# Turning the queries and keys of local attention: a product with the identity in place of the transposing instruction

## The chip, the cores and the metric

The kernel runs on one core of a Trainium2 chip. A core has a matrix engine (TensorE; PE in the profile, with its loads of the stationary operand shown apart as PEld), a vector engine (DVE), an activation engine (ACT), a general engine (POOL) and DMA queues, of which SP issues most here. The metric is the device time of one execution in microseconds.

## The reference, cut to what matters

One layer of a hybrid encoder: a normed input is projected, and three groups of heads work on it side by side, a chunked state-space scan, attention in a window, and attention to a memory. Their outputs are joined and projected back. There are two sequences, of 1024 and of 256 tokens, with 2048 features, handled as ten tiles of 128 tokens. The part that matters here is the attention in a window, with 8 query heads and 2 key heads of 64 features:

```python
q = rms_norm(q.reshape(b, T, ATT_HEADS, ATT_HEAD_DIM), q_norm_g)
k = rms_norm(k.reshape(b, T, ATT_KV_HEADS, ATT_HEAD_DIM), k_norm_g)
...
s = jnp.einsum('bnqgrd,bnkgd->bngrqk', qb, kw).astype(jnp.float32) * (d ** -0.5)
...
logits = jnp.where(valid[:, None, None], s - slopes[None, :, :, None, None] * dist[:, None, None], -jnp.inf)
...
o = jnp.einsum('bngrqk,bnkgd->bnqgrd', probs.astype(v.dtype), vw)
```

The sum over d needs the features of q and k on the partitions, while the projection leaves tokens there. So each tile of q and of k has to be turned.

## The kernel before

The large projections run all through the kernel: weight tiles are fetched, split into a rounded high part and a rounded low part by `wsplit` (L206 on ACT, L207 on DVE), and multiplied in the rounded kind (type `F32R`), three products for each pair of parts. `block_tok` (L258 to L260) has tokens on the output's partitions, `block_feat` (L293 to L295) features, with 320 moving columns, and `block_pair` (L1268 to L1270) saves products by sums of parts.

The smaller work is written as generators: `k_prep` for a tile's keys, `attn` for a tile's window attention, `mem_attn`, `ssd_up`, `ssd_down` and so on. They stand in two lanes; after each step of a projection, `pump` takes so many steps from the lanes, by the rates in `RATES`. That is the order in which the program is written down. The order in which each engine then gets its instructions is made by a planner of the language from this order, from the priorities that the kernel gives (`tc.high_priority`, `tc.issue_after`), from the buffers that are free and from the planner's own costs of instructions.

`k_prep(t)` fetches a tile's keys, norms them and writes `kh`: 128 partitions by 4 x 2 x 64, the high part of each key head twice side by side and the low part twice, all in the rounded type (L528, L530). Then four turns of 128 x 128 (L536) fill one bank `pk`, and `kT` (high, L539 on DVE) and `kL` (low, L540 on ACT) are copied from it. `attn(t)` does the same for queries: for each of the two key heads it writes `qh` (L647, L648: high and low part of four query heads, side by side), turns it in four instructions (L653) into the bank `pq`, and copies it to `qT` (L655 on ACT). In `scores` (L671, L672) one product takes the turned high and low part of a query together, as 128 rows, against the doubled high part of the keys, and a second one against the low part.

`identr` is the 128 x 128 identity in the rounded type. Other turns of the kernel use the same transposing instruction: in the rounded type L744, L853, L889, L1074 and L1088, in the unrounded type L449, L610, L611, L693, L794 and L1038. Unrounded products are in `values` (L703, L809), in the sums of `dt_prep` (L590 to L592) and in `diag` (L970).

Of the kernel before, what the change touches and what calls it, by code (L numbers as in the profile page):

```python
# [11 lines left out]
F32R = mybir.dt.float32r  # L12
# [7 lines left out]
P = 128  # L20
# [24 lines left out]
def hymba_encoder_kernel(  # L45
# [7 lines left out]
    V, A, G, T, S = nc.vector, nc.scalar, nc.gpsimd, nc.tensor, nc.sync  # L53
# [23 lines left out]
    def const(shape, name, dtype=F32):  # L77
        return cp.tile(shape, dtype, tag=name, name=name)
# [4 lines left out]
    def psum(name):  # L83
        return mix.tile([P, 512], F32, tag="mix", name=name)


    identr = const([P, P], "identr", F32R)
# [34 lines left out]
    def rsqrt(dst, src, scale, n):  # L122
        G.tensor_scalar(out=dst, in0=src, scalar1=scale, scalar2=EPS, op0=ALU.mult, op1=ALU.add)
        G.tensor_tensor(out=dst, in0=dst, in1=mhalf[:, :n], op=ALU.pow)

    def hv(ap, n=8):
        return ap.rearrange("p (h d) -> p h d", h=n)

    def hb(ap, n, d):
        return ap.unsqueeze(2).broadcast_to([P, n, d])  # L130
# [284 lines left out]
    def w2(name):  # L415
        return mp.tile([P, 512], F32, tag="wa", name=name, bufs=WA)
# [86 lines left out]
    def taken(name, t):  # L503
        return fetched.pop((name, t)) if (name, t) in fetched else fetch[name](t)

    def fetch_next():

        name = lanes[0][1][0] if len(lanes[0]) > 1 else ("", 0)
        if name[0] in fetch:
            fetched[name] = fetch[name[0]](name[1])  # L510

    def k_prep(t):
        r = taken("k_prep", t)
        yield
        ss = sm.tile([P, 2], F32, tag="s2", name="kss", bufs=4)
        sq = w2("ksq")[:, :P]
        A.activation(sq, r, AF.Square)
        V.reduce_sum(out=ss, in_=hv(sq, 2), axis=AX.X)
        rr = sm.tile([P, 2], F32, tag="s2", name="krr", bufs=4)
        rsqrt(rr, ss, 1.0 / 64, 2)  # L520
        yield
        r3 = hv(r, 2)
        V.tensor_mul(r3, r3, hb(rr, 2, 64))
        V.tensor_mul(r3, r3, gq.unsqueeze(1).broadcast_to([P, 2, 64]))

        kh = mp.tile([P, 4, 2, 64], F32R, tag="wa", name="kh", bufs=WA)
        for d in range(2):
            A.activation(kh[:, 0:2, d, :], r3, AF.Copy)  # L528
        for d in range(2):
            V.tensor_sub(kh[:, 2:4, d, :], r3, kh[:, 0:2, 0, :].bitcast(F32))  # L530
        yield
        yield
        ps = psum("pk")
        kf = kh.rearrange("p a b d -> p (a b d)")
        for a in range(4):
            T.transpose(ps[:, a * P:(a + 1) * P].bitcast(F32R), kf[:, a * P:(a + 1) * P], identr)  # L536
        sl = t if t < 5 else t - 3
        c = slice(sl * P, (sl + 1) * P)
        V.tensor_copy(kT[:, :, c], hv(ps[:, :256], 2))  # L539
        A.activation(kL[:, :, c], hv(ps[:, 256:], 2), AF.Copy)  # L540
        fetch_next()
        yield
# [77 lines left out]
    def attn(t):  # L620
# [23 lines left out]
        for b in range(2):  # L644
            qh = mp.tile([P, 4, 2, 64], F32R, tag="wa", name="qh", bufs=WA)
            qb = q3[:, 4 * b:4 * b + 4, :]
            A.activation(qh[:, :, 0, :], qb, AF.Copy)  # L647
            V.tensor_sub(qh[:, :, 1, :], qb, qh[:, :, 0, :].bitcast(F32))  # L648
            yield
            ps = psum("pq")  # L650
            qf = qh.rearrange("p a b d -> p (a b d)")
            for a in range(4):
                T.transpose(ps[:, a * P:(a + 1) * P].bitcast(F32R), qf[:, a * P:(a + 1) * P], identr)  # L653
            o = mp.tile([P, 512], F32R, tag="qT", name="qT", bufs=2)
            A.activation(o, ps, AF.Copy)  # L655
            qT.append(o)
# [826 lines left out]
    def refill_o(grp, when):  # L1483
        def f(k):
            if k not in when:
                return []
            q = when[k]
            need((attn, mem_attn, ssd_down, ssd_down)[q], range(grp * 5, grp * 5 + 5))
            return [part(fill_direct, q, j, oT_d[q][grp][:, j, :],
                         gain=None if q < 2 else vec[:, R_SG + 4 * (q - 2) + j:R_SG + 4 * (q - 2) + j + 1])  # L1490
                    for j in range(4)]
        return f
# [76 lines left out]
    for u, unit in enumerate(units):  # L1569
# [43 lines left out]
    run(block_tok(w_kv, 5, ev_dtkv(0), before_last=lambda _: need(vectors, [0])), RATES[0]["kv"], hold=5,  # L1613
        extra=lambda k: some_left() if left else None)
    queue(0, k_prep, range(5))
    queue(0, attn, range(4))
    queue(1, dt_prep, [0])

# [22 lines left out]
    def gate(name, c, after=None):  # L1641
        for b in range(2):
            feat(name, b, ev_gateT(c, 1, 2 * b), 1, after if b else None)

    need(attn, range(4))
    kv_shift()
    run(block_tok(w_kv, 5, ev_dtkv(5)), RATES[1]["kv"], extra=lambda k: some_left() if left else None)
    queue(0, k_prep, range(5, 10))
    queue(0, attn, [4])
    queue(1, dt_prep, [5])  # L1650
# [110 lines left out]
```

## Time and profile before

| what | value |
|---|---|
| median of 3 runs | 1787.72 us (1787.32 to 1790.27) |
| span of the profiled execution, first to last instruction | 1784.2 us |
| PE busy | 1774.6 us, 10838 products |
| PEld busy | 1606.3 us |
| DVE busy | 1245.8 us |
| ACT busy | 921.5 us |
| POOL busy | 547.3 us |
| the four turns of L536, L653 | 40 records of 238 ns mean, 80 of 246 ns mean |

The page lists busy time by engine, then the span in slices, the DMA queues, the chain of work that ended last and the costliest groups of instructions. "L653 PE MATMUL pq<-identr,qh" means line 653 of the kernel, run on PE, that writes the tile `pq` from `identr` and `qh`. Records of the matrix engine overlap: the length of a product's record contains the way through the array, so what one costs in a stream is read from the distance of the starts and not from the lengths.

### The profile page before, as it was taken

To read this page: it belongs to the slowest core of one execution; us is meant where nothing else is said; L and a number is where in the kernel's file an instruction comes from. 1 tells how busy PE (TensorE), PEld (TensorE's weight loads), DVE (VectorE), ACT (ScalarE), POOL (GpSimd) and SP (SyncE) were. 2 spreads that over 40 slices of the span, in tenths; PEclk is the share of its full clock that TensorE was granted. 3 is DMA by queue.
4 is the path that set the end of the run, shared out by engine and by line. 5 is a ranking of instruction groups with operands and counts; after the bars stand their busy time and mean duration, and the time that the engine had idled before them with its cause. 6 is when DMAs were issued, how large, how long until landed. Compare 5 with 4: busy or idle time off the path is not lost.

```text
span 1784.2 us, 31407 instructions
## 1 busy us (share of the span) xinstructions
PE 1774.6 (99%) x10838; PEld 1606.3 (90%) x10838; DVE 1245.8 (70%) x2358; ACT 921.5 (52%) x2049; POOL 547.3 (31%) x900
## 2 busy tenths in 40 slices
PE   9999999999999999999999999999999999999999
PEld 7889999999998999999889977877988888899999
DVE  5596788888768887777665666557777644766665
ACT  5555455555434766756464565544447533533333
POOL 0105789999810100001001010000100000057775
PEclk9999999999999999999999999999999999999999
DMA  8654454445446644453635645557777764744442
GB/s 299 191 183 125 135 154 148 141 146 159 126 144 205 199 134 139 135 162 110 189 118 175 193 148 160 168 158 249 229 229 242 247 189 140 224 147 142 148 142 78
DMA packets 208207, 301.12 MB, mean 169 GB/s; under 512 B 19568, under 2 KB 86192, under 8 KB 208048
## 3 DMA queue, kind: packets, MB, share of 16 engines
q1 hardware_dynamic: 207904, 299.06, 54.5%
q8 instruction: 85, 1.39, 0.3%
q14 instruction: 74, 0.61, 0.1%
q10 hardware_dynamic: 144, 0.06, 0.0%
HBM read 236.36 MB, written 62.69 MB: 168 GB/s over the span
## 4 chain that ended last, share of the span: by engine, by line
PE 82%; issue 6%; DVE 4%; DMA 4%; POOL 2%; ACT 1%; SPq 0%; POOLq 0%; ACTq 0%; DVEq 0%
PE acc L258 9%; PE acc L260 8%; PE acc L259 8%; PE acc L1268 7%; PE acc L1270 7%; PE acc L1269 7%; PE acc L293 5%; PE acc L295 5%; PE acc L294 5%; PE accm L1268 3%; PE accm L1269 3%; PE accm L1270 3%; PE po L703 1%; PE ppt L693 1%; PE py L970 1%
## 5 line engine op out<-in xcount | busy, mean ns | idle before, releaser
L207 DVE TENSOR_TENSOR wl<-wraw,wh 128x512 fp32r<-128x512 f32 (+1 forms) x480 | 346.2, 723 | 244.0 <-ACT wh L206 238.5
L206 ACT ACTIVATE wh<-wraw 128x512 fp32r<-128x512 f32 (+1 forms) x480 | 292.2, 613 | 312.4 <-PE acc L260 147.8
L258 PE MATMUL acc<-wh,xH 128*128 128x512 f32 (+1 forms) x1088 | 418.9, 385 | 0.4 <-DVE v_all L337 0.4
L260 PE MATMUL acc<-wh,xL 128*128 128x512 f32 (+1 forms) x1088 | 410.1, 377 | 0.0
L259 PE MATMUL acc<-wl,xH 128*128 128x512 f32 (+1 forms) x1088 | 409.7, 377 | 0.0
L258 PEld LDWEIGHTS acc<-wh,xH 128*128 128x128 f32 x1088 | 204.5, 188 | 37.8 <-issue 3.4
L260 PEld LDWEIGHTS acc<-wh,xL 128*128 128x128 f32 x1088 | 204.4, 188 | 37.0 <-issue 0.2
L259 PEld LDWEIGHTS acc<-wl,xH 128*128 128x128 f32 x1088 | 204.7, 188 | 35.9 <-issue 1.6
L293 PE MATMUL acc<-xH,wh 128*128 128x320 f32 x640 | 202.8, 317 | 0.0
L294 PE MATMUL acc<-xL,wh 128*128 128x320 f32 x640 | 198.8, 311 | 0.0
L295 PE MATMUL acc<-xH,wl 128*128 128x320 f32 x640 | 198.0, 309 | 0.0
L206 ACT ACTIVATE sh<-ws 128x384 fp32r<-128x384 f32 x176 | 91.3, 523 | 204.8 <-POOL ws L1236 102.5
L207 DVE TENSOR_TENSOR sl<-ws,sh 128x384 fp32r<-128x384 f32 x176 | 123.8, 706 | 94.6 <-ACT sh L206 94.4
L1236 POOL TENSOR_TENSOR ws<-wraw 128x128 f32<-128x128 f32 x176 | 110.8, 630 | 205.8 <-DMA wraw<-in_w_in_pairs_dram 80.9
L665 POOL COPY lg<-nsink 128x2 f32<-128x2 f32 x40 | 13.6, 340 | 379.1 <-PE ppt L693 221.3
L1236 POOL TENSOR_TENSOR ws<-wraw,ws 128x128 f32<-128x128 f32 x176 | 118.7, 674 | 13.8
L293 PEld LDWEIGHTS acc<-xH,wh 128*128 128x128 f32 x640 | 120.2, 188 | 2.8 <-issue 2.2
L294 PEld LDWEIGHTS acc<-xL,wh 128*128 128x128 f32 x640 | 120.3, 188 | 1.7 <-issue 1.4
L295 PEld LDWEIGHTS acc<-xH,wl 128*128 128x128 f32 x640 | 120.2, 188 | 0.6 <-issue 0.5
L1236 POOL TENSOR_TENSOR wraw<-wraw 128x128 f32<-128x128 f32 x176 | 112.9, 642 | 13.7
L1236 POOL TENSOR_TENSOR ws<-ws,wraw 128x128 f32<-128x128 f32 x176 | 115.6, 657 | 0.0
L362 DVE SCALAR_TENSOR_TENSOR c<-u,vec,c 128x638 f32<-128x638 f32 (+1 forms) x96 | 90.0, 938 | 9.9 <-ACT c L357 9.5
(437 smaller groups left out, 3942.7 us busy)
## 6 DMA issues: line engine op xcount, KB each, us to landing
wraw<-in_w_in_laid_dram SPq DMA_DIRECT2D x176, 256.0 KB, 3.0
wraw<-in_w_in_pairs_dram SPq DMA_DIRECT2D x112, 256.0 KB, 2.7
wraw<-in_w_out_laid_dram SPq DMA_DIRECT2D x64, 256.0 KB, 3.5
wraw<-in_w_out_pairs_dram SPq DMA_DIRECT2D x64, 256.0 KB, 2.8
rf<-ac SPq DMA_DIRECT2D x40, 256.0 KB, 4.1
rb<-ac SPq DMA_DIRECT2D x40, 256.0 KB, 4.7
wraw<-in_w_mem_laid_dram SPq DMA_DIRECT2D x32, 256.0 KB, 4.4
xst<-in_x_sample_dram SPq DMA_DIRECT2D x20, 256.0 KB, 5.9
```

Of the source, the lines that this page charges most:

```text
L206: a = A.activation(h, raw, AF.Copy)
L207: b = V.tensor_sub(l, raw, h.bitcast(F32))
L258: T.matmul(ps[t][:, :n], sh, h[:, :n], start=(k_ == 0), stop=False)
L259: T.matmul(ps[t][:, :n], sh, l[:, :n], start=False, stop=False)
L260: T.matmul(ps[t][:, :n], sl, h[:, :n], start=False, stop=(k_ == KT - 1))
L293: T.matmul(o, sh, cur["H", q][:, m, c], start=(k == 0), stop=False)
L294: T.matmul(o, sh, cur["L", q][:, m, c], start=False, stop=False)
L295: T.matmul(o, sl, cur["H", q][:, m, c], start=False, stop=(k == KT - 1))
L1236: G.tensor_tensor(out=o, in0=x, in1=y, op=op)
L1268: T.matmul(ps[p], h, xh, start=(k_ == 0), stop=False)
L1269: T.matmul(ps[p], h, xl, start=False, stop=False)
L1270: T.matmul(ps[p], l, xh, start=False, stop=(k_ == 7))
```

## The change

Eight instructions of the text, two loops over four, are written in another way: in place of the transposing instruction stands an ordinary product with `kf` or `qf` as stationary operand and the identity as moving operand. The result goes to the bank in its own type, so that the type is no longer reinterpreted. Data, tiles, copies behind it and all other turns of the kernel stay.

```diff
@@ k_prep
         ps = psum("pk")
         kf = kh.rearrange("p a b d -> p (a b d)")
         for a in range(4):
-            T.transpose(ps[:, a * P:(a + 1) * P].bitcast(F32R), kf[:, a * P:(a + 1) * P], identr)
+            T.matmul(ps[:, a * P:(a + 1) * P], kf[:, a * P:(a + 1) * P], identr, start=True, stop=True)
         sl = t if t < 5 else t - 3
@@ attn
             ps = psum("pq")
             qf = qh.rearrange("p a b d -> p (a b d)")
             for a in range(4):
-                T.transpose(ps[:, a * P:(a + 1) * P].bitcast(F32R), qf[:, a * P:(a + 1) * P], identr)
+                T.matmul(ps[:, a * P:(a + 1) * P], qf[:, a * P:(a + 1) * P], identr, start=True, stop=True)
             o = mp.tile([P, 512], F32R, tag="qT", name="qT", bufs=2)
```

## The prediction

> **What bounds the kernel now.** I read the page's first parts, then the busy time in stretches of 100 us over the part of the span in which the two edited lines run, then those lines themselves.
>
> ```profile
> span 1784.2 us, 31407 instructions
> PE 1774.6 (99%) x10838; PEld 1606.3 (90%) x10838; DVE 1245.8 (70%) x2358; ACT 921.5 (52%) x2049; POOL 547.3 (31%) x900
> PEclk9999999999999999999999999999999999999999
> ```
>
> ```profile
> 500.00:600.00 100.00, 99.31 (x575) 88.26 (x574) 81.73 (x174) 50.30 (x118) 13.34 (x20) 1.00 0.64 190
> 600.00:700.00 100.00, 99.51 (x693) 93.35 (x693) 79.11 (x180) 66.34 (x168) 9.56 (x15) 1.00 0.48 147
> 700.00:800.00 100.00, 99.96 (x721) 93.43 (x720) 75.19 (x171) 61.44 (x149) 8.04 (x14) 1.00 0.50 149
> 800.00:900.00 100.00, 98.74 (x674) 90.44 (x673) 70.14 (x162) 54.64 (x141) 7.88 (x9) 1.00 0.49 144
> 900.00:1000.00 100.00, 99.94 (x633) 90.58 (x632) 66.21 (x142) 58.89 (x154) 8.23 (x16) 1.00 0.49 155
> 1000.00:1100.00 100.00, 100.00 (x570) 81.69 (x569) 62.13 (x139) 58.09 (x141) 9.69 (x16) 1.00 0.54 171
> 1100.00:1200.00 100.00, 100.00 (x527) 79.89 (x526) 55.98 (x131) 53.03 (x133) 8.26 (x17) 1.00 0.52 161
> 1200.00:1300.00 100.00, 98.94 (x612) 83.60 (x610) 73.72 (x162) 47.00 (x115) 9.02 (x24) 1.00 0.73 231
> ```
>
> The columns after the length are the busy time of PE, PEld, DVE, ACT and POOL, then the granted clock. PE is idle for 0.69 + 0.49 + 0.04 + 1.26 + 0.06 + 0 + 0 + 1.06 = 3.6 us of these 800 us, while DVE never passes 82 and ACT never passes 67 of 100. So PE sets the pace through the whole stretch, and what one instruction adds to PE's stream is added to the end. But a busy PE says little of an instruction's price, since records overlap. The price of an instruction is the distance between starts, so I go to the order of time.
>
> ```profile
> L536 PE MATMUL pk<-identr,kh x40: 222/233/282, 565.2 to 1000.1; 128*128 128x128 f32 x40
> L653 PE MATMUL pq<-identr,qh x80: 221/247/627, 624.2 to 1269.3; 128*128 128x128 f32 x80
>   ACT qT L655: 0.3, 1
> ```
>
> The edit touches 40 + 80 = 120 instructions, between 565 and 1269 us. The last row is from the list of those that waited for L653: one wait of 0.3 us in all, so the copies behind the turns have slack and a later turn of some tenths of a us starts no chain there. In time one group of four turns looks like this:
>
> ```profile
> 623.62 0.31 PE L295 MATMUL acc<-xH,wl 128*128 128x320 f32 x1
> ...
> 624.06 0.31 PE L295 MATMUL acc<-xH,wl 128*128 128x320 f32 x1
> 624.21 0.46 PE L653 MATMUL pq<-identr,qh 128*128 128x128 f32 x4
> 624.50 0.38 PE L293 MATMUL acc<-xH,wh 128*128 128x320 f32 x1
> 624.72 0.30 PE L294 MATMUL acc<-xL,wh 128*128 128x320 f32 x1
> 624.86 0.31 PE L295 MATMUL acc<-xH,wl 128*128 128x320 f32 x1
> ```
>
> The columns are start, length, engine, line and so on. Undisturbed, products of 320 columns start 0.147 us apart (three steps from 623.62 to 624.06, and 0.15 from 624.06 to 624.21). From 624.06 to 624.72 there are 0.66 us; two such products account for 0.294 of them, so four turns cost 0.366 us, **0.091 us each**, and that includes the longer step behind them (0.22 in place of 0.147).
>
> **The change part by part.** It removes 120 turns in the transposing kind and adds 120 ordinary products with the data as stationary part and the rounded identity of 128 columns as moving part. Instruction count, operands, output tile and the copies that read it stay (L539, L540, L655 read the same 512 columns); no DMA, no wait and no engine is added. So there are two terms: the price of 120 products, and what the planner, which orders each engine's instructions by its own idea of their cost, does with a different instruction.
>
> First term. No ordinary rounded product with 128 moving columns stands in the trace, so it is bounded by neighbours. What differs in the records is the load of the stationary part:
>
> ```profile
> L653 PEld LDWEIGHTS pq<-identr,qh 128*128 128x128 f32 x80 | 8.4, 140 | 1.4 <-issue 0.5
> L294 PEld LDWEIGHTS acc<-xL,wh 128*128 128x128 f32 x640 | 120.3, 188 | 1.7 <-issue 1.4
> L809 PEld LDWEIGHTS pmo<-mpT,mv 128*128 128x128 f32 x160 | 19.5, 191 | 0.9 <-ACT mpT L798 0.3
> ```
>
> A load takes 140 ns in the transposing kind, 188 in the rounded ordinary one, 191 in the unrounded one. The next rows say what that does to the distance of starts when the moving part is short.
>
> ```profile
> 834.75 0.29 PE L259 MATMUL acc<-wl,xH 128*128 128x288 f32 x1
> 834.88 0.30 PE L260 MATMUL acc<-wh,xL 128*128 128x288 f32 x1
> 835.02 1.05 PE L809 MATMUL pmo<-mpT,mv 128*128 128x128 f32 x8
> 835.83 0.38 PE L258 MATMUL acc<-wh,xH 128*128 128x288 f32 x1
> 836.04 0.29 PE L259 MATMUL acc<-wl,xH 128*128 128x288 f32 x1
> ```
>
> ```profile
> 878.09 0.35 PE L590 MATMUL pacs<-e,upper 128*128 128x80 f32 x2
> 878.28 0.39 PE L591 MATMUL pacs<-e,lower 128*128 128x80 f32 x2
> 878.50 0.48 PE L592 MATMUL pacs<-e,one 128*128 128x160 f32 x2
> ```
>
> ```profile
> 821.08 0.28 PE L772 MATMUL pms<-mkH,mqh 128*128 128x256 f32 x1
> 821.19 0.28 PE L773 MATMUL pms<-mkL,mqh 128*128 128x256 f32 x1
> 821.30 0.28 PE L774 MATMUL pms<-mkH,mql 128*128 128x256 f32 x1
> ```
>
> Unrounded products take two records each in this trace. Eight records of L809 cost 836.04 - 834.88 - 2 x 0.13 = 0.90 us, 0.1125 each, with 128 columns; two of L591 take 0.22, so 0.11 each, with only 80 columns. The same price at 80 and at 128 columns means that it isn't the columns but the load that sets it: an ordinary load of 128 columns holds the next product back for 0.11 us. Rounded products with 256 columns are 0.11 apart too. I take 0.1125 for the new product: it is nearest to L809, which has its shape. Then each of the 120 costs 0.1125 - 0.091 = 0.0215 us more, and all of them **2.6 us** more.
>
> Ends of this term. Low: if loads were hidden, 128 columns would stream. The rows above give 0.147 us for 320 columns, so 0.46 ns a column and 0.059 us for 128; 120 x (0.059 - 0.091) = **-3.8 us**. High: if a rounded product of so few columns goes at the unrounded rate, it costs two records of L809, 0.225 us; 120 x (0.225 - 0.091) = **+16.1 us**.
>
> The Trainium skill, "Perfetto Trace Analysis", section "Transposes", says that a logical transpose should be a transpose rather than a standard matmul, since transposes have special logic that skips the arithmetic. This speaks against the change, and the load rows (140 against 188 ns) agree in direction. The Trainium skill, "TensorE: Matmul & The Clock Gate", section "Back-to-back issue gap", gives some 81 ns for a sustained pair of load and product with 128 columns. By that figure the 120 would come out as an estimate of 120 x (0.081 - 0.091) = -1.2 us; the rows with 0.11 us in this case's trace are against it.
>
> Second term. That the order is not that of the text shows here, where other work's data came late for half a group:
>
> ```profile
> 577.35 0.29 PE L536 MATMUL pk<-identr,kh 128*128 128x128 f32 x2
> 577.96 0.36 PE L536 MATMUL pk<-identr,kh 128*128 128x128 f32 x2 [0.33 <-DVE kh L530]
> ```
>
> Here the engine stood at the third turn for 0.33 us until DVE had made its low parts. Everything up to the first turn keeps its place. Behind it the planner may place attention, scan and weight work otherwise, and PE's idle time is drawn anew. If all of it vanished in the 800 us, -3.6 us. If each of the eight stretches became as bad as the worst (1.26), 8 x 1.26 - 3.6 = +6.5 us. The present order is one of many and I have no row to place the new one, so I take the middle, **+1.4 us**.
>
> Sum: 2.6 + 1.4 = +4.0 us. The profiled span is 1784.2 us and would become 1788.2. The median of the runs, 1787.72, is 3.5 us above that span (start and end outside the first and last instruction), and nothing here touches those 3.5 us. So 1787.72 + 4.0 = **1791.7 us**.
>
> **The rivals.**
> (A) The slow rate: a rounded product with 128 moving columns costs as much as an unrounded one, +16.1 us, and with the planner's middle 1805.2. For it: no rounded product under 256 columns stands in the kernel, so no row excludes it. Against it: rounded rows of 256, 288 and 320 columns step with their columns at one record each, with no sign of a cliff.
> (B) Faster: the loads of the four products run under the streaming of the one before, so that they step by their columns. Place: inside the 30 groups of four; price 0.059 us a product, -3.8 us, 1783.9 with the order as it is. It decides from the point at which a product costs less than the turn's 0.091. For it speaks this row:
>
> ```profile
> 618.68 1.97 PE L970 MATMUL py<-rb,xs 128*64 128x128 f32 x32
> ```
>
> ```profile
> L970 PE MATMUL py<-rb,xs 128*64 128x128 f32 x320 | 19.6, 275 | 0.0
> ```
>
> With 0.275 us for the last record alone, that is (1.97 - 0.275) / 31 = 0.055 us a record with 128 moving columns. Against it: these load 64 columns, half as many, and two halves of the array take turns; with 128 loaded columns every row says 0.11. A load hidden only in part gives a price between 0.059 and 0.1125, and at 0.091 nothing is won or lost. The 81 ns that the Trainium skill gives in "TensorE: Matmul & The Clock Gate", section "Back-to-back issue gap", would be such a part.
> (C) Nothing is changed: the builder turns a product with the identity into the same instruction, or the load still goes in 140 ns. Then 1787.7. Against it: the edit leaves out what asks for the transposing kind.
>
> **How the numbers follow.** Forecast with load-bound products 0.60, A 0.22, B 0.13, C 0.05. The forecast alone lies between 1787.72 + 2.6 - 3.6 = 1786.7 and 1787.72 + 2.6 + 6.5 = 1796.8. The range of 8 in 10 goes from 1785, which leaves out most of B, to 1806, which holds A with the planner's middle but not with its bad end. A measurement of this kernel tells about 0.2% from no change, 3.6 us, so the borders are 1784.1 and 1791.3. Of the forecast's 0.60 I put 0.34 above the upper border (its middle is 0.4 us over it), 0.23 between and 0.03 below (an order better than I priced). A is slower, 0.22; B is 0.10 below and 0.03 between; C is between, 0.05. In sum faster 0.13, same 0.31, slower 0.56.
>
> **What would show it.** In the changed profile the loads of L536 and L653 should be 188 ns in place of 140. A group of four should cost 0.45 us by the same subtraction of starts around it, not 0.366; 0.9 would be A, 0.24 B. Their records should still be 40 and 80; twice as many would be A. The granted clock should stay 1.00. The part of the trace ahead of the first turn at 565.2 us should be the same to some tenths of a us; if the first big difference is elsewhere, the planner did it. PE's idle time between 500 and 1300 us should lie between 0 and 10 us; more of it means that the second term, not the first, was mis-sized. The forecast is wrong if a group costs 0.45 us and the time still differs by more than 9 us.

## The result and the profile after

The changed kernel takes 1793.05 us in the median of 7 runs (1791.75 to 1794.17), the kernel before 1787.64 us (1785.10 to 1790.27): 1.0029 of it, with an interval of 1.0019 to 1.0039. That is 5.4 us more, where 4.0 us were forecast. The profiled execution's span is 1792.3 us, 8.1 us more than the one of before; this execution took 1794.06 us, so it is one of the longer ones, while the 1784.2 us of before is one of the shorter (other executions of that kernel span 1783.0 to 1790.1 us).

First the page's head, then the busy time by stretches of 100 us (columns as before), with the sum over 500 to 1300 us:

```profile
span 1792.3 us, 31408 instructions
PE 1777.8 (99%) x10838; PEld 1609.5 (90%) x10838; DVE 1244.3 (69%) x2358; ACT 920.6 (51%) x2049; POOL 546.7 (31%) x900
```

```profile
600.00:700.00 100.00, 98.30 (x679) 93.02 (x677) 76.25 (x173) 62.98 (x161) 9.63 (x14) 1.00 0.45 141
700.00:800.00 100.00, 98.97 (x710) 92.36 (x710) 76.65 (x174) 63.10 (x153) 8.13 (x15) 1.00 0.50 147
...
sum 800.00, PE 792.78 PEld 698.77 DVE 557.30 ACT 445.56 POOL 74.62; mean PE 99.10 PEld 87.35 DVE 69.66 ACT 55.69 POOL 9.33
```

PE's idle time in these 800 us is 800 - 792.78 = 7.2 us, against 3.6 before. Number of products and granted clock are the same. So something besides the products' own price was added: waits.

The edited instructions, by line and then one group in order of time:

```profile
L653 PEld LDWEIGHTS pq<-identr,qh 128*128 128x128 f32 x80 | 10.9, 190 | 1.0 <-issue 0.2 <-ACT fh L910 0.2
L536 PEld LDWEIGHTS pk<-identr,kh 128*128 128x128 f32 x40 | 5.7, 190 | 0.3
```

```profile
625.56 0.31 PE L295 MATMUL acc<-xH,wl 128*128 128x320 f32 x1
625.71 0.56 PE L653 MATMUL pq<-identr,qh 128*128 128x128 f32 x4
626.10 0.36 PE L293 MATMUL acc<-xH,wh 128*128 128x320 f32 x1
626.30 0.31 PE L294 MATMUL acc<-xL,wh 128*128 128x320 f32 x1
```

The load of the stationary part is 190 ns in place of 140, still in one record for each product. By the subtraction used before, the group costs 626.30 - 625.56 - 0.294 = 0.446 us in place of 0.366. That is 0.111 us a product and **0.020 us more than a turn**; 120 of them make 2.4 us.

The waits of PE that grew against the first profile of before, longest in total first (us in total, times, longest; the rows left out stand in both lists at about the same size, but for one at L1091, 0.6 and now 1.0):

```profile
...
PE psc L671 <- ACT qT L655: 1.3, 2, 1.0
...
PE pst L896 <- ACT fh L910: 1.1, 1, 1.1
...
PE acc L293 <- DVE zs L309: 0.9, 2, 0.7
PE psc L671 <- DVE xs L891: 0.7, 1, 0.7
```

Not all of them come from the change. The second profile of the unchanged kernel, taken for the experiments below, has two of them as well:

```profile
PE pst L896 <- ACT fh L910: 1.3, 1, 1.3
...
PE psc L671 <- DVE xs L891: 0.5, 1, 0.5
```

The other two, for L655 and for L309, are 0.2 us and nothing in the first profile of before, and below 0.1 us in the second. The first of them is the clearest. Here it is on PE and on ACT, after and then before:

```profile
778.61 1.00 PE L653 MATMUL pq<-identr,qh 128*128 128x128 f32 x8
...
779.94 0.31 PE L293 MATMUL acc<-xH,wh 128*128 128x320 f32 x1
781.21 0.44 PE L671 MATMUL psc<-kT,qT 128*128 128x384 f32 x1 [0.96 <-ACT qT L655]
```

```profile
779.33 0.39 ACT L396 ACTIVATE u<-acc 128x256 f32<-128x256 f32 x1
779.75 0.93 ACT L357 ACTIVATE c<-u,vec 128x646 f32<-128x646 f32 x1
780.58 1.06 ACT L655 ACTIVATE qT<-pq 128x512 fp32r<-128x512 f32 x2
```

```profile
775.80 0.39 ACT L396 ACTIVATE u<-acc 128x256 f32<-128x256 f32 x1
776.06 1.10 ACT L655 ACTIVATE qT<-pq 128x512 fp32r<-128x512 f32 x2
777.02 0.96 ACT L357 ACTIVATE c<-u,vec 128x646 f32<-128x646 f32 x1
```

Before, ACT copied the turned queries right after the evacuation of L396 (its copy out of the bank) and did the convolution's first tap (L357, 0.96 us) later. Now the tap stands first. The copies begin 1.25 us after the start of L396 in place of 0.26, so 1.0 us later, and PE stands at the first score product for 0.96 us. The turned data had been there: the eight products ended at 778.61 + 1.00 = 779.61, before ACT began the tap at 779.75. It is the order that makes the wait, not the length of the products.

### The profile page after: what moved, and what is told of

It is laid out like the page before. It is cut to its first block, busy times and chain, and to the rows that moved or that the text cites. A ratio compares the mean times of both kernels' runs of the same rounds, so it can differ in the third digit from the quotient of the medians.

```text
span 1792.3 us, 31408 instructions
## 1 busy us (share of the span) xinstructions
PE 1777.8 (99%) x10838; PEld 1609.5 (90%) x10838; DVE 1244.3 (69%) x2358; ACT 920.6 (51%) x2049; POOL 546.7 (31%) x900
## 4 chain that ended last, share of the span: by engine, by line
PE 79%; issue 7%; DVE 6%; DMA 5%; ACT 2%; POOL 1%; SPq 0%; ACTq 0%; DVEq 0%; POOLq 0%
PE acc L258 8%; PE acc L260 8%; PE acc L259 8%; PE acc L1270 7%; PE acc L1268 7%; PE acc L1269 7%; PE acc L293 4%; PE acc L295 4%; PE acc L294 4%; PE accm L1269 3%; PE accm L1268 3%; PE accm L1270 3%; PE po L703 1%; DVE wl L207 1%; PE ppt L693 1%
## 5 line engine op out<-in xcount | busy, mean ns | idle before, releaser
L260 PE MATMUL acc<-wh,xL 128*128 128x512 f32 (+1 forms) x1088 | 410.1, 377 | 0.0
L260 PEld LDWEIGHTS acc<-wh,xL 128*128 128x128 f32 x1088 | 204.4, 188 | 37.1 <-issue 0.2
L1236 POOL TENSOR_TENSOR wraw<-wraw 128x128 f32<-128x128 f32 x176 | 111.7, 635 | 13.7
```

The lines of the kernel that those rows point to most:

```text
L260: T.matmul(ps[t][:, :n], sl, h[:, :n], start=False, stop=(k_ == KT - 1))
L1236: G.tensor_tensor(out=o, in0=x, in1=y, op=op)
```

## The experiments

Theory 1: a product costs 0.0205 us more than a turn, as seen in the starts around the groups, and the rest of the 5.4 us is waits that the planner's other order makes. Theory 2: all of it is the price of the products, 0.045 us each, partly hidden from the starts. To tell them apart I measured, beside the times, the stretch from the first turn of keys to the last turn of queries, which contains all that the edit touches. The rows quoted give the starts of first and last of each line.

**How well the stretch repeats.** Both kernels again, unchanged.

> The kernel before, profiled a second time, to see how far the stretch from the first turn of keys to the last turn of queries repeats. Theory 1: 704.1 us, give or take 1 us. If it moves by 3 us or more, the waits read from single profiles are no evidence.

> The changed kernel, timed and profiled a second time. Theory 1: the stretch from the first turn of keys to the last turn of queries takes 711.2 us, give or take 1 us, of which 2.4 us are price; the time is 1.0024 to 1.0034 of the kernel before. The wait of PE for the copy L655 in tile 3 is there again.

```profile
L536 PE MATMUL pk<-identr,kh x40: 222/233/254, 568.0 to 1002.9; 128*128 128x128 f32 x40
L653 PE MATMUL pq<-identr,qh x80: 221/247/627, 626.3 to 1272.4; 128*128 128x128 f32 x80
```

```profile
L536 PE MATMUL pk<-identr,kh x40: 222/274/279, 564.6 to 1004.0; 128*128 128x128 f32 x40
L653 PE MATMUL pq<-identr,qh x80: 221/274/625, 624.5 to 1274.6; 128*128 128x128 f32 x80
```

Before: 1272.4 - 568.0 = 704.4 us, and 1269.3 - 565.2 = 704.1 in the first profile. After: 710.0, and 1276.6 - 565.4 = 711.2 in the first. So the stretch repeats within about 1 us, although its beginning moved from 565.2 to 568.0 in one and the same kernel; the 710.0 is just outside the 711.2 give or take 1 that was expected. The changed kernel is 6.3 us longer there in the mean. The price is 2.4 us by the group of four shown above; a group of eight behind L260 gives 0.024 us a product by the same subtraction (1.16 us before, from 1065.61 to 1066.77, and 1.35 after, from 1071.53 to 1072.88), which would make 2.9 us. PE's idle time inside the stretch (its length less PE's busy time) is 2.8 and 3.6 us in the two profiles of before and 6.6 and 5.7 in those of the changed kernel, 2.9 more in the mean. The last 0.5 to 1.0 us are longer steps between products; which ones they are stays open. Its time was 1794.35 us, 1.0032 (1.0023 to 1.0041) of the kernel before, and the wait for L655 was there again with 1.0 us. The waits for L655 and L309 make some 2 of the 2.9 us.

**Which turns change the order.** Each of the 30 groups of four was changed alone, and the compiled order of all engines compared with the order before (these compiled orders aren't among the runs here). Eleven groups of queries change nothing in any order, also together. This gives two kernels that share out the 120 products. In their traces PE, ACT and POOL run the same sequence of instructions as the kernel before in the one, and the same as the changed kernel in the other. The first of them (one line, broken here for reading; the keys keep the transposing instruction):

```diff
-T.transpose(ps[:, a * P:(a + 1) * P].bitcast(F32R), qf[:, a * P:(a + 1) * P], identr)
+(T.matmul(ps[:, a * P:(a + 1) * P], qf[:, a * P:(a + 1) * P], identr, start=True, stop=True)
+ if (t, b) in ((0, 0), (2, 0), (5, 0), (5, 1), (6, 0), (6, 1), (7, 0), (7, 1), (8, 0), (9, 0), (9, 1))
+ else T.transpose(ps[:, a * P:(a + 1) * P].bitcast(F32R), qf[:, a * P:(a + 1) * P], identr))
```

> 44 of the 120 turns (eleven groups of attention tiles 0, 2 and 5 to 9) are ordinary products, 76 stay transposing; every engine's order of instructions is that of the kernel before. Theory 1 (a product costs 0.0205 us more than a turn, as the starts around the groups say, and the rest of the change is waits that the new order makes): +0.9 us, no new wait on PE. Theory 2 (all of the 5.4 us is the price of 120 products, 0.045 us each, part of it not seen in the starts): +2.0 us.

> The other 76 turns are ordinary products (all ten key tiles, nine groups of queries), 44 stay transposing; PE, ACT, POOL and SP have the order of the changed kernel. Theory 1: 76 x 0.0205 = 1.6 us and nearly the whole of the waits, 2.5 to 3.5 us, so +4 to +5 us, with waits of PE at the same places as in the changed kernel. Theory 2: 76 x 0.045 = +3.4 us, without them.

With the order kept, then with the order moved:

```profile
L536 PE MATMUL pk<-identr,kh x40: 222/233/254, 568.3 to 1003.0; 128*128 128x128 f32 x40
L653 PE MATMUL pq<-identr,qh x80: 221/252/625, 626.5 to 1273.1; 128*128 128x128 f32 x80
```

```profile
L536 PE MATMUL pk<-identr,kh x40: 222/274/279, 566.7 to 1006.1; 128*128 128x128 f32 x40
L653 PE MATMUL pq<-identr,qh x80: 221/251/627, 626.9 to 1276.2; 128*128 128x128 f32 x80
```

The busy time of PE over these two stretches (length, then PE):

```profile
568.28:1273.14 704.86, 702.04 (x4398) 617.46 (x4396) 488.80 (x1086) 405.68 (x1015) 63.89 (x111) 1.00 0.54 164
566.74:1276.18 709.44, 703.48 (x4398) 618.11 (x4396) 489.51 (x1086) 406.42 (x1015) 65.06 (x111) 1.00 0.53 163
```

Order kept: 704.8 us, 0.5 us more than the mean of before; 44 products are 0.9 us of price, and PE's idle time is 2.8 us, as in the kernel before, so no wait is left over. The time is 1.0007 (0.9998 to 1.0016) of before, 1.3 us more by this ratio. Order moved: 709.5 us, 5.2 us more, of which 76 products are 1.6 us; of the 3.6 us above the price, 2.8 are idle time of PE (6.0 us, against 3.2 in the mean of before). The time is 1.0024 (1.0015 to 1.0033), 4.3 us more. Theory 2 wanted 2.0 and 3.4 us in the stretch and got 0.5 and 5.2. The times alone could not decide, for both theories lie within the intervals; the stretches do.

**Keys alone and queries alone.** One of the two changed lines each.

> Only the keys' 40 turns (L536) are ordinary products. Theory 1: 0.8 us of price, and the waits that come with the keys' part of the new order: +0.8 to +4 us. Theory 2: 40 x 0.045 = +1.8 us.

> Only the queries' 80 turns (L653) are ordinary products. Theory 1: 1.6 us of price, and the waits that come with the queries' part of the new order: +1.6 to +5 us; with the run of the keys alone, the parts above the price add up to the 3 us of the whole change. Theory 2: 80 x 0.045 = +3.6 us.

```profile
L536 PE MATMUL pk<-identr,kh x40: 222/274/278, 568.6 to 1005.8; 128*128 128x128 f32 x40
L653 PE MATMUL pq<-identr,qh x80: 221/247/627, 628.3 to 1275.3; 128*128 128x128 f32 x80
```

```profile
L536 PE MATMUL pk<-identr,kh x40: 222/233/254, 566.0 to 1003.8; 128*128 128x128 f32 x40
L653 PE MATMUL pq<-identr,qh x80: 221/274/625, 625.0 to 1274.4; 128*128 128x128 f32 x80
```

Keys: 706.7 us, 2.4 more than before, 0.8 of it price; 1.0009 (1.0001 to 1.0018). Queries: 708.4 us, 4.1 more, 1.6 of it price; 1.0029 (1.0018 to 1.0040). The parts above the price are 1.6 and 2.5 us; their sum, 4.1, is near the whole change's 6.3 - 2.4 = 3.9. Theory 2 would have 1.8 and 3.6, which these two runs don't exclude.

**One place alone.** Only the eight turns of attention tile 3, the ones in front of the wait shown above, are products. The compiled order of ACT then differs from the one before in this alone:

```
 L396 ACTIVATE u<-acc 128x256
+L357 ACTIVATE c<-u,vec 128x646
 L655 ACTIVATE qT<-pq 128x512 x2
-L357 ACTIVATE c<-u,vec 128x646
```

> Only the eight turns of attention tile 3 are ordinary products. The order of instructions differs from that of the kernel before at this place alone: on ACT the first tap of a convolution (L357) stands ahead of the two copies of the turned queries (L655), and on PE a score product (L671) stands one projection product earlier. Theory 1: 8 x 0.0205 = 0.16 us of price, and a wait of PE of about 0.95 us at L671 for the copy L655, as in the changed kernel at 781.21 us; from the first turn of keys to the last turn of queries 1.1 us more than before. Theory 2 (price only): 8 x 0.045 = 0.4 us and no such wait.

```profile
L536 PE MATMUL pk<-identr,kh x40: 222/233/254, 564.3 to 1000.1; 128*128 128x128 f32 x40
L653 PE MATMUL pq<-identr,qh x80: 221/248/627, 622.6 to 1269.2; 128*128 128x128 f32 x80
...
776.46 0.44 PE L671 MATMUL psc<-kT,qT 128*128 128x384 f32 x1 [0.96 <-ACT qT L655]
```

The same wait, 0.96 us to the hundredth, came from eight products. It stands in all six profiles in which ACT has the tap ahead of the copies and the group of turns is eight products of 128 columns, and in none of the four in which ACT copies first (both of before, order kept, keys alone). The stretch is 704.9 us, 0.65 more than the mean of before, where 1.1 were expected; the difference is within what a stretch repeats to. The kernel was run once (1786.21 us), too little for so small a difference in time. So at this place the price of these eight, 0.16 us, is a sixth of the wait that their order makes; what that wait costs the whole kernel this run doesn't show, since its idle time in the stretch, 3.6 us, is no more than in the second profile of before.

**Is it the load?** Each turn is made of two products of 64 moving columns, with the same 128 columns loaded for both; the keys' line is changed alike.

```diff
-T.matmul(ps[:, a * P:(a + 1) * P], qf[:, a * P:(a + 1) * P], identr, start=True, stop=True)
+[T.matmul(ps[:, a * P + j:a * P + j + 64], qf[:, a * P:(a + 1) * P], identr[:, j:j + 64], start=True, stop=True) for j in (0, 64)]
```

> Each of the 120 turns is made of two ordinary products with 64 moving columns each, with the same 128 columns loaded for both. Theory 1 (the load sets the price): 0.11 us for each of the 240, a group of eight costs about 0.9 us in place of 0.45, and the kernel takes 120 x 0.1125 = 13.5 us more than the changed one, about 1806.5 us, give or take 4 us for another order. Rival (the moving columns set it): a group costs about 0.45 us, and the time is that of the changed kernel, 1793 us, give or take 4 us.

```profile
627.73 0.31 PE L295 MATMUL acc<-xH,wl 128*128 128x320 f32 x1
627.88 0.97 PE L653 MATMUL pq<-identr,qh 128*128 128x64 f32 x8
628.69 0.39 PE L293 MATMUL acc<-xH,wh 128*128 128x320 f32 x1
628.91 0.31 PE L294 MATMUL acc<-xL,wh 128*128 128x320 f32 x1
```

A group of eight costs 628.91 - 627.73 - 0.294 = 0.886 us, 0.111 for each product of 64 columns, the same as for 128. So the moving columns don't set the price; twice as many loads cost twice as much. That it is the load, and not some other fixed price of an ordinary product, is argued from the records: a turn and a product move the same 128 columns and differ there in the load, 140 against 190 ns. The time is 1801.56 us, 1.0074 (1.0056 to 1.0092) of before, 13.7 us more; the price of 240 products in place of 120 turns is 240 x 0.111 - 120 x 0.0915 = 15.7 us. The stretch says it more sharply: 1286.2 - 566.4 = 719.8 us, 15.6 more than the mean of before. Theory 2's price, 0.0915 + 0.045 us a product, would have made 240 x 0.1365 - 120 x 0.0915 = 21.8 us.

The forecast for this run, 1806.5 us give or take 4, was missed by 0.9 us below its range, for it carried the waits of the changed kernel along, and PE's list of waits has none for L655 here. That isn't because ACT has another order in tile 3; the tap stands ahead of the copies here too (ACT, then PE):

```profile
782.57 0.39 ACT L396 ACTIVATE u<-acc 128x256 f32<-128x256 f32 x1
782.99 0.93 ACT L357 ACTIVATE c<-u,vec 128x646 f32<-128x646 f32 x1
783.82 1.06 ACT L655 ACTIVATE qT<-pq 128x512 fp32r<-128x512 f32 x2
...
781.85 1.87 PE L653 MATMUL pq<-identr,qh 128*128 128x64 f32 x16
784.45 0.45 PE L671 MATMUL psc<-kT,qT 128*128 128x384 f32 x1
```

From the first turn to the first score product it is 784.45 - 781.85 = 2.60 us, and in the changed kernel 781.21 - 778.61 = 2.60 too. ACT sets the moment at which the queries are there; with twice as many products PE is busy in the time in which it otherwise stands. So against the changed kernel some 0.9 us of price cost nothing there, since they take the place of the wait. PE's idle time in the whole stretch is 719.9 - 716.8 = 3.1 us, against 6.1 in the mean of the changed kernel.

**More of the same.** The other 240 turns of the rounded type (L744, L853, L889, L1074, L1088) are products too.

```diff
-T.transpose(ps[:, j * P:(j + 1) * P].bitcast(F32R), ld[g][3][:, j, :], identr)
+T.matmul(ps[:, j * P:(j + 1) * P], ld[g][3][:, j, :], identr, start=True, stop=True)
...
```

> The other 240 turns of the rounded type (L744, L853, L889, L1074, L1088) are ordinary products too; their data are not rounded before, so the products drop their low bits. Theory 1: 240 x 0.0205 = 4.9 us more price than in the changed kernel, and between -3 and +6 us of waits by another order: 1795 to 1804 us, 1798 at the same waits. Theory 2 (0.045 us for each): +10.8 us, 1803.8 us.

```profile
PE pd L1074 <- DVE y L1093: 3.3, 2, 3.1
PE pxs L889 <- ACT mpr L781: 3.2, 1, 3.2
PE psc L671 <- ACT qT L655: 1.3, 2, 1.0
```

1812.27 us in the median of four runs (1806.37 to 1813.52), 1.0129 (1.0107 to 1.0151): 24 us more than before, over both theories. But three of the four had a mean granted clock of 0.996 or 0.997, and these are the three at 1811.52 us and above; the fourth, which is the profiled one, had 1.000, and its 1806.37 us are still over both. So some 6 us of the 24 go with the clock. The six executions of before next to them had 1.000; whether the change brings the lower clock isn't shown. The profiled execution's span is 1804.6 us, 20.4 more than the first of before. PE is busy for 1783.6 us of it, 9.0 more than before, where 360 products are 7.4 us of price by the 0.0205; the other 11.4 us are idle time. Two waits of 3 us, of which the first profile of before has only 0.5 us (at L1074), are 6 of them; the rest are smaller waits. My bound of 6 us for waits by another order was too small.

## Why the prediction was right

The direction and the range held: +4.0 us forecast, +5.4 measured, 1793.05 inside 1785 to 1806, and the class with the largest chance, slower by over 0.2%, is the one that came. The range is wide, though, since it had to hold rival A. The price of the products is the part that was understood. That the sum came so near is in part luck: about half of the measured 5.4 us or more came from the second term, and that term was a middle between two bounds, without a row that spoke for its size or its sign.

Point by point. That PE sets the pace, so that each added piece is added to the end: the eleven groups that only add price (order kept) lengthened the stretch by 0.5 us for 0.9 us of price, and the halves by 15.6 for 15.7. The first term: 0.1125 us for a product was taken from L809 and 0.111 was measured; 0.091 for a turn stood; so 2.6 us forecast, 2.4 to 2.9 found. The reading that a product of 80 columns costs as much as one of 128 was right: at 64 columns it is 0.111 too. Rival A (the unrounded rate, 0.9 us a group) is excluded by the group of 0.446 us, rival B (hidden loads, 0.24 us a group) too, and rival C by the loads of 190 ns. The row of L970 was no evidence for B: in the single records of the trace its products start in pairs, 7 ns apart, with 0.11 us from pair to pair, so the 0.055 us is half of what a pair costs and shows no hidden load of 128 columns.

The second term was the weak one. The middle of -3.6 and +6.5, 1.4 us, stood in the sum, and 3.9 us of the stretch (2.9 of it idle time of PE), or 5.4 - 2.4 = 3.0 us by the times, was measured. The place was right in kind (PE's idle time in 500 to 1300 us rose from 3.6 to 7.2 us, inside the 0 to 10 named), but the step mis-sized is the middle: it treated the present order as one among many, while the runs with another order were mostly worse: keys alone, queries alone, order moved and all turns each lengthen the stretch or the span beyond their price; the halves don't, in part because the longer products fill a wait. With all turns changed the idle time grew by 11.4 us, beyond the upper bound of 6.5. Also "the copies behind the turns have slack" read the wrong side: the 0.3 us is what ACT's copy waited for the turns, and at the place shown the turns were indeed done before ACT came to the copy. What counted is how long PE waits for the copy, and there the slack is gone as soon as other work stands ahead of it on ACT: where the planner put 0.93 us of it, PE waited 0.96 us.

Two smaller readings were off without a bearing on the sum. The 3.5 us between span and time are not all start and end: in every other run that lists both it is 1.7 to 1.8 us, and the rest is that the profiled execution was a short one. And that the part ahead of the first turn stays the same (565.2 us, then 565.4) is no sign of anything, for it moves to 568.0 in the unchanged kernel.

What stays open: why the planner gives L357 the first place is inferred, from the fact that the turning instruction alone was changed; its own costs were not looked at. Of the 3 to 4 us above the price, about 1 us is shown with a cause (tile 3). The waits for L309 (0.9 and 0.5 us in the changed kernel, none before) and the second one for L655 come with the new order too, but were not made alone. The wait for L910 is no part of it, as it lies behind the stretch and is there in the unchanged kernel; that for L891 is 0.5 us there and 0.7 in the changed one. The last 0.5 to 1.0 us stay unplaced.

## What to carry to other kernels

A turn of a 128 x 128 block is best left to the transposing instruction where the result allows it: here the difference went with the load of the stationary part and didn't shrink with the moving columns. Where a planner orders the instructions, an edit of a few instructions also buys a new order, and in a kernel with a saturated engine that can cost more than the instructions themselves; compare the compiled orders, find the edits that leave them alone, and price the two parts separately. Measure a difference of a few us by a stretch between two fixed instructions as well as by the time. Profile the unchanged kernel twice before you put a wait down to an edit, for a wait that one profile lacks may stand in the next.

## What the runs showed of the hardware that was not expected

The same program reaches its first turn of keys at 565.2 us in one execution and at 568.0 in another, while the following 704 us repeat to 0.3 us. The granted clock goes with it. Here are 10 us of the second profile of before, then of the first; the clock is the third number from the end:

```profile
150.00:160.00 10.00, 9.10 (x48) 8.58 (x49) 5.34 (x10) 6.83 (x15) 3.02 (x5) 0.83 0.64 184
150.00:160.00 10.00, 9.18 (x63) 8.92 (x62) 6.18 (x11) 7.55 (x16) 4.02 (x6) 1.00 0.62 192
```

From 152.5 to 155.8 us the clock is 0.50 in the second profile and 1.00 in the first. The three profiles with such a dip (this one, order kept and keys alone) begin the stretch at 568.0 to 568.6 us, the eight without it at 564.3 to 566.7. Inside the stretch all have 1.00. What sets the dip off, no run shows.

Rounded products with 128 or 64 moving columns show no slower rate of their own in these runs: the price is 0.111 us for both. The Trainium skill's rule in "Perfetto Trace Analysis", section "Transposes", to use the transposing instruction and not a standard matmul, is borne out here: 0.0915 against 0.111 us.
